# Product-key expert layer: own rooms for stored results, an earlier gate load, later index casts and one later exponential

## The chip, the cores and the metric

The kernel runs on one core of a Trainium2 chip. The metric is the device time of one execution in microseconds (us); the kernel before takes 2628.84 us, the median of 3 runs (2627.95 to 2629.35).

## The reference

The program is two transformer blocks on 512 tokens of width 1024. The change lies in the second half of the first block, the product-key layer (`peer_ffn`), which picks 16 of 16384 single-neuron experts per head and token:

```python
q = (xt @ w_query).reshape(T, H, 2, PEER_HALF)
s = jnp.einsum('thpd,hpkd->thpk', q, sub_keys).astype(f32)
top_s, top_i = lax.top_k(s, K)
cand_s = (top_s[:, :, 0, :, None] + top_s[:, :, 1, None, :]).reshape(T, H, K * K)
...
best_s, best_pos = lax.top_k(cand_s, K)
expert_idx = jnp.take_along_axis(cand_i, best_pos, axis=-1)
gate = jax.nn.softmax(best_s, axis=-1)
...
act = jnp.einsum('td,ted->te', x_blk, u[i_blk]).astype(f32)
hid = jax.nn.gelu(act, approximate=False) * g_blk
return jnp.einsum('te,ted->td', hid.astype(v.dtype), v[i_blk])
```

There are 8 heads, 128 keys for each half of a key, K = 16, and 16384 rows of 1024 in `u` and in `v`.

## The kernel before

The kernel is written in the order in which each engine executes (its schedule is manual): every engine takes its instructions strictly in program order, and waits where an operand or a room (a buffer of a pool) is not free yet. A DMA is issued from the queue of the engine that names it: `nc.sync` is SP, `nc.scalar` is ACT, `nc.gpsimd` is POOL.

**Weights.** Large matmuls are made of three: each operand is split into a high part and a rest, and `mm3` (L226 to L228) computes hi*hi, lo*hi and hi*lo. The class `Ring` brings the weights: `load` (L47, SP) fills one of 3 rooms `w_raw`, `split` copies the high part on ACT (L59, `w_hi`) and subtracts for the rest (L69, `w_lo`) on DVE, or on POOL where `pool=True`. A room of `w_raw` is free for the next load when `w_lo` has been computed. With `later=True` the subtraction is kept back until the next call of `next` or `split`.

**Tokens 128 to 511** (three tiles of 128) go the dense way: for each of the 128 blocks of 128 experts, a *u block* of 24 matmuls 128x384 gives the activations of all experts of the block (`act_steps`, 4 steps of 6 matmuls), ACT takes their gelu out of PSUM (L863), and later the expert loop multiplies by a dense gate and by the rows of `v`. Tokens 0 to 127 gather their experts' rows instead.

**`routes`** has three parts. (1) The query projection: 16 blocks on PE, each followed by `rank(b)`: 4 small matmuls of queries and keys into a PSUM tile `sm` of which there are two (L921), then DVE finds the 16 best with their indices (L924 to L932), and POOL casts the indices `ti` to `tib` (L933). (2) `choose(t, h0, h1)`: DVE works out the 16 best pairs of a head (21 pieces for 4 heads), with an exponential on ACT (L979) and, at the end, the indices `ik` (L1034). (3) `dispatch(t)` for t = 1, 2, 3: PE transposes `ik` and the gates (L1043 to L1045), and 32 rounds of one-hots and 8 matmuls each (L1081) build the dense gates, which ACT copies out of PSUM (L1082) and writes to DRAM in 24 writes `gd<-h` (L1088). `choose` of the next tile is woven between the rounds.

To keep PE busy, u blocks are fed in between: `steps(n)` adds n to an account and runs that many steps of u blocks. There are 4 steps between the last two ranks, 1.2 per piece of `choose(1, 4, 8)`, 2 + 32 x 1.2 in each `dispatch`. What is left of the 43 fed blocks is run at the end of `routes` (`drain(u_x)`), then two more. The results of the first 8 blocks go to `rows`, of the next 26 to `ge`, and of the last 11 to a tile `ga` of 2 rooms in `routes`' own pool `r_wk`, from which POOL writes them to DRAM (`away<-ga`, L866).

**`experts`** starts with a new pool `e_wk` in the space that `routes` gave back: POOL clears `acc` (L1143) and issues the load of the first gate tile, 1536 KB (`gate_tile(0)`, `gg<-gd`, L1147). `hidden(b)` multiplies gelu and gate on DVE (`hg`, L1187), splits the product into `hh` on ACT (L1188) and `hl` on DVE (L1189), and block b's 18 matmuls `o` read them.

Of the kernel before, what the change touches and what calls it, by code (L numbers as in the profile page):

```python
# [11 lines left out]
F32 = mybir.dt.float32  # L12
# [3 lines left out]
U32 = mybir.dt.uint32  # L16
# [6 lines left out]
NT = 4  # L23
# [5 lines left out]
class Ring:  # L29
# [49 lines left out]
    def next(self, ahead=2, pool=False, later=False):  # L79
        i = self.pos  # L80
        self.flush()
        self.load(i + self.depth)
        self.split(i + 1 + ahead, pool, later)
        self.pos += 1
        return self.hl.pop(i)
# [138 lines left out]
def mm3(nc, out, a, b, start, stop):  # L224

    nc.tensor.matmul(out, a[0], b[0], start=start, stop=False)  # L226
    nc.tensor.matmul(out, a[0], b[1], start=False, stop=False)  # L227
    nc.tensor.matmul(out, a[1], b[0], start=False, stop=stop)  # L228
# [12 lines left out]
def proj_fm(k, ps, nblk, xT, evac, pool=False, cuts=1):  # L241

    nc = k.nc
    for b in range(nblk):
        hi, lo = (w.rearrange("p (c f) -> p c f", c=KD) for w in k.ring.next(pool=pool, later=cuts > 1))
        p = ps.tile([128, T], F32, name="mm")
        for c in range(KD):
            mm3(nc, p, (hi[:, c], lo[:, c]), xT(c), c == 0, c == KD - 1)
            if c < KD - 1 and (c + 1) % (KD // cuts) == 0:
                yield  # L250
                if c + 1 == 2 * (KD // cuts):
                    k.ring.flush()
        evac(b, p)
        yield
# [19 lines left out]
def by_row(xT):  # L274

    return lambda c: tuple(x[:, c, :] for x in xT)
# [19 lines left out]
def drain(*gens):  # L296
    for g in gens:
        for _ in g:
            pass
# [482 lines left out]
LAG = 27 + LEAD  # L782

AWAY = 10
N = 384
# [30 lines left out]
def peer(k, h, xT, pools, parts, first):  # L816


    nc, tc, A = k.nc, k.tc, k.A
    with ExitStack() as ctx:  # L820
        ep = lambda name, bufs, **kw: ctx.enter_context(tc.tile_pool(name=name, bufs=bufs, **kw))
        s = Peer()
        s.one = one = ep("p2_one", 1)
        s.gep = ep("p2_ge", LAG - LEAD + 1)
        s.gat = k.rows
        s.pa = pools[0]
        s.gd = ep("p2_dram", 1, space=DRAM).tile([16, 128, NCH, 8 * CH], F32, name="gd")
        s.hd = ep("p2_hd", 1, space=DRAM).tile([128, NT, D], F32, name="hd")
        away = [ep(f"p2_away{i}", 1, space=DRAM).tile([128, N], F32, name="away") for i in range(AWAY + 1)]
        s.xT = xT  # L830
        s.n0 = one.tile([128, D], F32, name="n0")
        s.idx = one.tile([128, 128], I32, name="idx")
        s.g0 = one.tile([128, 128], F32, name="g0")
        s.act0 = one.tile([128, 128], F32, name="act0")
        s.ge, s.nact = {}, 0

        def act_steps(later=False):

            n = s.nact
            if n == 128:  # L840
                return
            if n >= LAG - 1 and n - LAG + 1 in s.away:
                ge = s.gep.tile([128, N], F32, name="ge")
                nc.sync.dma_start(out=ge, in_=s.away.pop(n - LAG + 1))
                s.ge[n] = ge
                s.nact += 1
                return
            uh, ul = (x.rearrange("p (c i) -> p c i", c=KD) for x in k.ring.next(later=later))
            p = s.pa.tile([128, 512], F32, name="mm")
            for c in range(KD):  # L850
                mm3(nc, p[:, 0:N], (uh[:, c], ul[:, c]), (s.xT[0][:, c, 128:512], s.xT[1][:, c, 128:512]), c == 0, c == KD - 1)
                if c % 2 and c < KD - 1:
                    yield
            if s.nact < LEAD:

                if s.nact % 2 == 0:
                    s.two = s.gat.tile([128, D], F32, name="rows")
                ge = s.two[:, s.nact % 2 * N:s.nact % 2 * N + N]
            elif s.wk is not None and n >= LAG - 1:
                ge = s.wk.tile([128, N], F32, name="ga")  # L860
            else:
                ge = s.gep.tile([128, N], F32, name="ge")
            nc.scalar.activation(ge, p[:, 0:N], AF.Gelu)  # L863
            if s.wk is not None and n >= LAG - 1:
                s.away[n - LAG + 1] = away[n - LAG + 1]
                nc.gpsimd.dma_start(out=away[n - LAG + 1], in_=ge)  # L866
            else:
                s.ge[n] = ge
            s.nact += 1
        s.act_steps = act_steps  # L870
        s.act = lambda later=False: drain(act_steps(later))
        s.away, s.wk = {}, None
        with ExitStack() as c2:
            routes(k, h, c2, s, pools[1], first)
        s.wk, s.nact = None, LAG - 1
        parts[1].close()
        return experts(k, s)


def routes(k, h, c2, s, ps, first):  # L880
    nc, tc, A = k.nc, k.tc, k.A
    ep = lambda name, bufs, **kw: c2.enter_context(tc.tile_pool(name=name, bufs=bufs, **kw))
    r1 = ep("r_one", 1)
    s.wk = wk = ep("r_wk", 2)
    s1 = ep("r_sm", 2, space=PSUM)
    s2 = ep("r_g", 2, space=PSUM)
    xT = s.xT
# [9 lines left out]
    for b in range(0, 16, 3):  # L897
        kt = s.gep.tile([128, 3, 128], F32, name="ge")
        n = min(3, 16 - b)
# [9 lines left out]
    tib = r1.tile([128, NT, 16, 16], BF, name="tib")  # L909
# [3 lines left out]
    def ev(b, p):  # L913
        qs[b] = wk.tile([128, T], F32, name="oa", bufs=4)
        nc.scalar.activation(qs[b], p, AF.Copy)

    def rank(b):
        q = qs.pop(b)
        sc = s1.tile([128, NT, 128], F32, name="sm")
        for t in range(NT):  # L920
            nc.tensor.matmul(sc[:, t, :], q[:, t * 128:(t + 1) * 128], keys[b], start=True, stop=True)  # L921
        rep = wk.tile([128, NT, 128], F32, name="ob", bufs=3)
        for t in range(NT):
            nc.vector.max(tv[:, t, b, 0:8], sc[:, t, :])  # L924
        for t in range(NT):
            nc.vector.match_replace(out=rep[:, t, :], in_to_replace=tv[:, t, b, 0:8], in_values=sc[:, t, :], imm_value=-3e38)
        for t in range(NT):
            nc.vector.max(tv[:, t, b, 8:16], rep[:, t, :])
        ti = wk.tile([128, NT, 16], U32, name="ti")
        for t in range(NT):  # L930
            nc.vector.max_index(ti[:, t, 0:8], tv[:, t, b, 0:8], sc[:, t, :])
            nc.vector.max_index(ti[:, t, 8:16], tv[:, t, b, 8:16], rep[:, t, :])  # L932
        nc.gpsimd.tensor_copy(tib[:, :, b, :], ti)  # L933
    gates, picks = {}, {}

    def choose(t, h0=0, h1=8, calm=None):
# [154 lines left out]
    def feed():  # L1091

        while s.nact < LAG + AWAY - 2:
            for i, _ in enumerate(s.act_steps()):
                if i == 1:
                    k.ring.split(k.ring.pos + 3, later=True)
                yield
            yield
    u_x, due = feed(), [0]

    def steps(n):
        due[0] += n
        while due[0] >= 1:
            due[0] -= 1
            next(u_x, None)


    for b in range(2):
        p, w = first[b]
        half_block(k, p, w, xT, 1)  # L1110
        ev(b, p)
        if b:
            rank(0)
    side = choose(1, 0, 4)
    for b, _ in enumerate(proj_fm(k, ps, 14, by_row(xT), lambda b, p: ev(b + 2, p), pool=True)):
        rank(b + 1)
        for _ in range(4 if b > 6 else 0):
            next(side, None)
    k.ring.split(k.ring.pos + 3, pool=True)
    steps(4)  # L1120
    rank(15)
    drain(side)
    for i, _ in enumerate(choose(1, 4, 8)):
        steps(1.2)
    for t in range(1, NT):
        calm = []
        weave(dispatch(t, calm), choose((t + 1) % NT, calm=calm), 1)
    drain(u_x)
    while s.nact < LAG + AWAY:
        s.act()  # L1130


def experts(k, s):
    nc, tc, A = k.nc, k.tc, k.A
    with ExitStack() as ctx:
        ep = lambda name, bufs, **kw: ctx.enter_context(tc.tile_pool(name=name, bufs=bufs, **kw))
        AHEAD, LAST, ROWS = 8, 125, 100 + LEAD
        wk = ep("e_wk", 2)
# [44 lines left out]
        def hidden(b):  # L1183
            ge = s.ge.pop(b)
            hg = wk.tile([128, N], F32, name="hg")
            hi, lo = (wk.tile([128, N], FR, name=n) if b <= LAST else s.gep.tile([128, N], FR, name="ge") for n in ("hh", "hl"))
            nc.vector.tensor_mul(hg.rearrange("p (c t) -> p c t", c=NCH), ge.rearrange("p (c t) -> p c t", c=NCH), gg[b // 8][:, :, b % 8, :])  # L1187
            nc.scalar.activation(hi, hg, AF.Copy)  # L1188
            nc.vector.tensor_sub(lo, hg, hi)  # L1189
            hid[b] = (hi, lo)  # L1190
        hidden(0)
        s.act()
        for b in range(LAST):
            if b % 8 == 2 and b < 120:
# [32 lines left out]
        for b in range(LAST + 1, 128):  # L1227
            hidden(b)
# [1010 lines left out]
```

## Time and profile before

| | |
|---|---|
| median of 3 runs | 2628.84 us |
| the profiled execution | 2629.32 us |
| its span | 2627.5 us |
| PE busy | 2561.2 us, 97% of the span |
| DVE busy | 1668.3 us, 63% |
| ACT busy | 940.1 us, 36% |
| POOL busy | 579.7 us, 22% |

The profile is one execution. A row of the timeline shows when an instruction started, how long it took, and in brackets how long its engine had been idle and which instruction released it. A stretch of the windows view shows busy time of every engine and the clock that TensorE (PE) was granted, 1.00 being 2.4 GHz and 0.50 being 1.2 GHz. With PE busy for nearly the whole span, time is found in the few places where it is idle or at the lower clock.

### The profile page before, as it was taken

How to read it: one execution, taken by the hardware profiler on the slowest of the kernel's cores; microseconds unless marked ns; L12 is line 12 of the kernel's file. 1: busy time of each engine (PE TensorE's matmuls, PEld its weight loads, DVE VectorE, ACT ScalarE, POOL GpSimd, SP SyncE). 2: the span in 40 equal slices, each digit the busy share in tenths (PEclk: the TensorE clock that was granted, in tenths of full speed). 3: DMA queues.
4: the chain of work that ended last, by engine and by line, in shares of the span. 5: the costliest groups of instructions: out<-in, count | busy, mean ns of one | idle time of the engine just before them, and what ended most of it. 6: DMA issues, size and time to landing. Idle time of an engine off the chain costs nothing.

```text
span 2627.5 us, 35859 instructions
## 1 busy us (share of the span) xinstructions
PE 2561.2 (97%) x13350; PEld 2037.8 (78%) x13350; DVE 1668.3 (63%) x3269; ACT 940.1 (36%) x1662; POOL 579.7 (22%) x485
## 2 busy tenths in 40 slices
PE   9999989997999999999999999999999999998997
PEld 7778889997789999999998778788888864453543
DVE  6446899993688887888888663555565552332223
ACT  5324237773333333333333443555422321110112
POOL 3200322222145555444443030111000110000000
PEclk9999999999999999999999999999999999999999
DMA  4223235666799999899898532222232579999996
GB/s 134 65 94 103 92 105 169 187 198 213 256 332 333 331 332 332 323 332 331 332 335 317 201 117 93 73 74 72 98 119 88 200 294 398 409 409 409 409 409 256
DMA packets 207952, 615.96 MB, mean 234 GB/s; under 512 B 18151, under 2 KB 69528, under 8 KB 205216
## 3 DMA queue, kind: packets, MB, share of 16 engines
q1 hardware_dynamic: 117808, 437.37, 44.8%
q0 software_dynamic: 38848, 142.71, 15.2%
q10 hardware_dynamic: 51120, 33.56, 4.4%
q8 instruction: 106, 1.74, 0.3%
q14 instruction: 70, 0.57, 0.1%
HBM read 579.95 MB, written 33.62 MB: 234 GB/s over the span
## 4 chain that ended last, share of the span: by engine, by line
PE 69%; DVE 4%; ACT 1%; DMA 1%; issue 1%; DVEq 0%; ACTq 0%; POOLq 0%; POOL 0%
PE mm L226 8%; PE mm L228 8%; PE mm L227 8%; PE o L226 6%; PE o L228 6%; PE o L227 6%; PE y L2035 4%; PE up L2014 4%; PE gate L2014 4%; PE pc L2046 2%; PE sc L226 1%; PE sc L227 1%; PE sc L228 1%; PE gate L1853 1%; PE up L1853 1%; PE po L1516 1%
## 5 line engine op out<-in xcount | busy, mean ns | idle before, releaser
L226 PE MATMUL mm<-nT_hi,w_hi 128*128 128x384 f32 (+1 forms) x1624 | 594.0, 366 | 2.4 <-ACT rows L863 2.3
L228 PE MATMUL mm<-nT_hi,w_lo 128*128 128x384 f32 (+1 forms) x1624 | 579.8, 357 | 2.7 <-POOL w_lo L69 2.7
L227 PE MATMUL mm<-nT_lo,w_hi 128*128 128x384 f32 (+1 forms) x1624 | 578.1, 356 | 0.0
L69 DVE TENSOR_TENSOR w_lo<-w_raw,w_hi 128x1024 fp32r<-128x1024 f32 x366 | 453.5, 1241 | 143.6 <-ACT w_hi L59 143.1
L59 ACT ACTIVATE w_hi<-w_raw 128x1024 fp32r<-128x1024 f32 x392 | 403.7, 1050 | 85.6 <-DMA w_raw<-in_peer_uT_dram 26.1
L226 PEld LDWEIGHTS mm<-nT_hi,w_hi 128*128 128x128 f32 x1624 | 306.4, 189 | 31.3 <-issue 3.6
L228 PEld LDWEIGHTS mm<-nT_hi,w_lo 128*128 128x128 f32 x1624 | 305.7, 188 | 28.0 <-POOL w_lo L69 3.7
L227 PEld LDWEIGHTS mm<-nT_lo,w_hi 128*128 128x128 f32 x1624 | 306.6, 189 | 24.8
L226 PE MATMUL o<-w_hi,hh 128*128 128x512 f32 x756 | 296.1, 392 | 17.9 <-ACT hh L1188 17.9
L228 PE MATMUL o<-w_hi,hl 128*128 128x512 f32 x756 | 297.6, 394 | 0.0
L227 PE MATMUL o<-w_lo,hh 128*128 128x512 f32 x756 | 296.7, 392 | 0.0
L863 ACT ACTIVATE ge<-mm 128x384 f32<-128x384 f32 x109 | 53.3, 489 | 429.3 <-PE mm L228 429.3
L226 PEld LDWEIGHTS o<-w_hi,hh 128*128 128x128 f32 x756 | 142.6, 189 | 48.3 <-ACT hh L1188 20.9
L228 PEld LDWEIGHTS o<-w_hi,hl 128*128 128x128 f32 x756 | 142.4, 188 | 31.9 <-DVE hl L1189 2.1
L227 PEld LDWEIGHTS o<-w_lo,hh 128*128 128x128 f32 x756 | 142.4, 188 | 28.0
L1189 DVE TENSOR_TENSOR hl<-hg,hh 128x384 fp32r<-128x384 f32 x126 | 70.7, 561 | 128.4 <-ACT hh L1188 128.4
L2021 DVE SCALAR_TENSOR_TENSOR ncT<-up,tw,ncT 128x512 f32<-128x512 f32 x16 | 12.0, 751 | 175.0 <-PE up L2014 175.0
L1153 POOL DMA_INDIRECT rows<-in_peer_u_dram,idx x64 | 91.6, 1431 | 121.6 <-DVE rows L1160 81.2
L2041 DVE SCALAR_TENSOR_TENSOR yl<-y,tw,yh 128x512 fp32r<-128x512 f32 x32 | 24.0, 751 | 144.9 <-ACT yh L2038 144.1
L1153 POOL DMA_INDIRECT h<-in_peer_u_dram,idx x64 | 90.9, 1420 | 105.9 <-DVE h L1160 95.2
L1188 ACT ACTIVATE hh<-hg 128x384 fp32r<-128x384 f32 x126 | 65.5, 519 | 134.3 <-DVE hg L1187 95.5
L1153 POOL DMA_INDIRECT h<-in_peer_v_dram,idx x64 | 82.6, 1291 | 106.2 <-DVE acc L1165 88.5
(732 smaller groups left out, 4680.4 us busy)
## 6 DMA issues: line engine op xcount, KB each, us to landing
w_raw<-in_peer_uT_dram SPq DMA_DIRECT2D x128, 512.0 KB
w_raw<-in_peer_v_dram SPq DMA_DIRECT2D x128, 512.0 KB
gd<-h ACTq DMA_DIRECT2D x24, 1024.0 KB
gg<-gd SPq DMA_DIRECT2D x15, 1536.0 KB
qk<-in_w_gate_dram SPq DMA_DIRECT2D x30, 512.0 KB
qk<-in_w_down_dram SPq DMA_DIRECT2D x28, 512.0 KB
qk<-in_w_up_dram SPq DMA_DIRECT2D x26, 512.0 KB
w_raw<-in_w_conv_dram SPq DMA_DIRECT2D x24, 512.0 KB
```

What stands on the lines that cost most here:

```text
L59: nc.scalar.activation(hi, w, AF.Copy)
L69: e.tensor_sub(lo, w, hi)
L226: nc.tensor.matmul(out, a[0], b[0], start=start, stop=False)
L227: nc.tensor.matmul(out, a[0], b[1], start=False, stop=False)
L228: nc.tensor.matmul(out, a[1], b[0], start=False, stop=stop)
L863: nc.scalar.activation(ge, p[:, 0:N], AF.Gelu)
L1153: nc.gpsimd.indirect_dma_start(out=r, out_offset=None, in_=A["peer_u"] if i < 128 else A["peer_v"], in_offset=bass.IndirectOffsetOnAxis(ap ...
L1188: nc.scalar.activation(hi, hg, AF.Copy)
L1189: nc.vector.tensor_sub(lo, hg, hi)
L1853: nc.tensor.matmul(p[:, i, 0:n], a[:, t, f], P[:, t, 0:n], start=i + t + j == 0, stop=t == NT - 1 and j == 1, skip_group_check=True)
L2014: nc.tensor.matmul(po[nm][r * 64:r * 64 + 64, :], xT[:, q * 2 + c, r * 64:r * 64 + 64], w[r][:, c * 512:c * 512 + 512], start=q == 0 and c ...
L2035: nc.tensor.matmul(py[i][r * 64:r * 64 + 64, :], aT[:, q, r * 64:r * 64 + 64], w[:, c * 512:c * 512 + 512], start=q == 0, stop=q == 3, ski ...
```

## The change

It has five parts.

- `ga` gets a pool of its own, `p2_ga`, with 2 rooms, that stays when `routes` ends. The flag `s.early` takes the place of the test on `s.wk`.
- The rest of the fed u blocks no longer runs at the end of `routes` but in `experts`, behind `gate_tile(0)`; `hidden(0)` stands ahead of the last u block.
- One u block more is fed among the ranks: 4 steps stand ahead of each of the ranks 14 and 15, where there were 4 steps between them only. For the two subtractions of weights in these steps `pool=s.slow` names POOL.
- The cast of rank b's indices is issued when rank b + 3 reaches its own (`turned(2)`), and the last three behind rank 15 (`turned()`); `ti` has 4 rooms.
- The exponential of `choose(1, 4, 8)` is kept back and issued two pieces later.

```diff
--- before.py
+++ after.py
@@ -823,6 +823,7 @@
         s.one = one = ep("p2_one", 1)
         s.gep = ep("p2_ge", LAG - LEAD + 1)
         s.gat = k.rows
+        ga = ep("p2_ga", 2)
         s.pa = pools[0]
         s.gd = ep("p2_dram", 1, space=DRAM).tile([16, 128, NCH, 8 * CH], F32, name="gd")
         s.hd = ep("p2_hd", 1, space=DRAM).tile([128, NT, D], F32, name="hd")
@@ -856,12 +857,12 @@
                 if s.nact % 2 == 0:
                     s.two = s.gat.tile([128, D], F32, name="rows")
                 ge = s.two[:, s.nact % 2 * N:s.nact % 2 * N + N]
-            elif s.wk is not None and n >= LAG - 1:
-                ge = s.wk.tile([128, N], F32, name="ga")
+            elif s.early and n >= LAG - 1:
+                ge = ga.tile([128, N], F32, name="ga")
             else:
                 ge = s.gep.tile([128, N], F32, name="ge")
             nc.scalar.activation(ge, p[:, 0:N], AF.Gelu)
-            if s.wk is not None and n >= LAG - 1:
+            if s.early and n >= LAG - 1:
                 s.away[n - LAG + 1] = away[n - LAG + 1]
                 nc.gpsimd.dma_start(out=away[n - LAG + 1], in_=ge)
             else:
@@ -869,10 +870,9 @@
             s.nact += 1
         s.act_steps = act_steps
         s.act = lambda later=False: drain(act_steps(later))
-        s.away, s.wk = {}, None
+        s.away, s.early = {}, True
         with ExitStack() as c2:
             routes(k, h, c2, s, pools[1], first)
-        s.wk, s.nact = None, LAG - 1
         parts[1].close()
         return experts(k, s)
 
@@ -881,7 +881,7 @@
     nc, tc, A = k.nc, k.tc, k.A
     ep = lambda name, bufs, **kw: c2.enter_context(tc.tile_pool(name=name, bufs=bufs, **kw))
     r1 = ep("r_one", 1)
-    s.wk = wk = ep("r_wk", 2)
+    wk = ep("r_wk", 2)
     s1 = ep("r_sm", 2, space=PSUM)
     s2 = ep("r_g", 2, space=PSUM)
     xT = s.xT
@@ -926,11 +926,18 @@
             nc.vector.match_replace(out=rep[:, t, :], in_to_replace=tv[:, t, b, 0:8], in_values=sc[:, t, :], imm_value=-3e38)
         for t in range(NT):
             nc.vector.max(tv[:, t, b, 8:16], rep[:, t, :])
-        ti = wk.tile([128, NT, 16], U32, name="ti")
+        ti = wk.tile([128, NT, 16], U32, name="ti", bufs=4)
+
+        turned(2)
         for t in range(NT):
             nc.vector.max_index(ti[:, t, 0:8], tv[:, t, b, 0:8], sc[:, t, :])
             nc.vector.max_index(ti[:, t, 8:16], tv[:, t, b, 8:16], rep[:, t, :])
-        nc.gpsimd.tensor_copy(tib[:, :, b, :], ti)
+        last.append((tib[:, :, b, :], ti))
+    last = []
+
+    def turned(but=0):
+        while len(last) > but:
+            nc.gpsimd.tensor_copy(*last.pop(0))
     gates, picks = {}, {}
 
     def choose(t, h0=0, h1=8, calm=None):
@@ -1093,7 +1100,7 @@
         while s.nact < LAG + AWAY - 2:
             for i, _ in enumerate(s.act_steps()):
                 if i == 1:
-                    k.ring.split(k.ring.pos + 3, later=True)
+                    k.ring.split(k.ring.pos + 3, pool=s.slow, later=True)
                 yield
             yield
     u_x, due = feed(), [0]
@@ -1113,21 +1120,28 @@
             rank(0)
     side = choose(1, 0, 4)
     for b, _ in enumerate(proj_fm(k, ps, 14, by_row(xT), lambda b, p: ev(b + 2, p), pool=True)):
-        rank(b + 1)
+        if b < 13:
+            rank(b + 1)
         for _ in range(4 if b > 6 else 0):
             next(side, None)
     k.ring.split(k.ring.pos + 3, pool=True)
-    steps(4)
-    rank(15)
+    s.slow = True
+    for b in (14, 15):
+        steps(4)
+        rank(b)
+    s.slow = False
+    turned()
     drain(side)
-    for i, _ in enumerate(choose(1, 4, 8)):
+    exps, n = [], 0
+    for _ in choose(1, 4, 8, exps):
+        n += len(exps)
+        if exps and n == 3:
+            exps.pop()()
         steps(1.2)
     for t in range(1, NT):
         calm = []
         weave(dispatch(t, calm), choose((t + 1) % NT, calm=calm), 1)
-    drain(u_x)
-    while s.nact < LAG + AWAY:
-        s.act()
+    s.u_x = u_x
 
 
 def experts(k, s):
@@ -1188,7 +1202,13 @@
             nc.scalar.activation(hi, hg, AF.Copy)
             nc.vector.tensor_sub(lo, hg, hi)
             hid[b] = (hi, lo)
+
+        drain(s.u_x)
+        while s.nact < LAG + AWAY - 1:
+            s.act()
         hidden(0)
+        s.act()
+        s.early, s.nact = False, LAG - 1
         s.act()
         for b in range(LAST):
             if b % 8 == 2 and b < 120:
```

The diff shows the code; the order of the instructions on POOL moves in two places. On **POOL at the last ranks** (the projection's end, up to the first one-hot of `dispatch(1)`; L933 is the cast of rank indices) before:

```order
L69 TENSOR_TENSOR w_lo<-w_raw,w_hi 128x1024
L933 CAST tib<-ti 128x4x16
L69 TENSOR_TENSOR w_lo<-w_raw,w_hi 128x1024
L933 CAST tib<-ti 128x4x16
L69 TENSOR_TENSOR w_lo<-w_raw,w_hi 128x1024
L933 CAST tib<-ti 128x4x16
L1064 TENSOR_TENSOR oa<-eq,pT 128x512 x46
```

and with the change (the cast is L940, the one-hot L1071):

```order
L69 TENSOR_TENSOR w_lo<-w_raw,w_hi 128x1024 x2
L940 CAST tib<-ti 128x4x16
L69 TENSOR_TENSOR w_lo<-w_raw,w_hi 128x1024
L940 CAST tib<-ti 128x4x16 x4
L69 TENSOR_TENSOR w_lo<-w_raw,w_hi 128x1024
L1071 TENSOR_TENSOR oa<-eq,pT 128x512 x44
```

Before, each subtraction stands behind the cast of the rank just issued, and the last one here belongs to u block 2; now the subtractions of u blocks 3 and 4 are POOL's too, and the last stands behind the casts of the ranks 12 to 15.

On **POOL at the end of `routes`** (L866 writes stored u results away, L1147 loads the first gate tile) before:

```order
L866 DMA away<-ga 128x384
L1064 TENSOR_TENSOR oa<-eq,pT 128x512
L866 DMA away<-ga 128x384 x9
L1143 MEMSET acc 128x1024
L1147 DMA gg<-gd 128x3072
L1153 DMA h<-in_peer_u_dram,idx 128x1024 x4
```

and with the change:

```order
L1071 TENSOR_TENSOR oa<-eq,pT 128x512
L867 DMA away<-ga 128x384
L1157 MEMSET acc 128x1024
L1161 DMA gg<-gd 128x3072
L867 DMA away<-ga 128x384 x7
L1167 DMA h<-in_peer_u_dram,idx 128x1024 x4
```

The clearing of `acc` and the gate load have moved ahead of seven of the eleven writes; the gathers of expert rows stay behind the last of them.

## Rows read from the trace of the kernel before

**Rows 1.** PE timeline: start us, duration us, engine, line, operation, [idle before <-releaser]

```profile
348.29 0.39 PE L228 MATMUL mm<-nT_hi,w_lo 128*128 128x512 f32 x1
...
350.23 1.13 PE L921 MATMUL sm<-ge,oa 128*128 128x128 f32 x8 [1.56 <-DVE ti L931]
...
351.12 0.42 PE L226 MATMUL mm<-nT_hi,w_hi 128*128 128x384 f32 x1
...
383.01 0.33 PE L226 MATMUL mm<-nT_hi,w_hi 128*128 128x384 f32 x1
...
387.17 0.33 PE L226 MATMUL mm<-nT_hi,w_hi 128*128 128x384 f32 x1
...
392.36 0.27 PE L1043 MATMUL mm<-ident,ik 128*128 128x128 f32 x1
```

**Rows 2.** Windows: stretch, its us, busy per engine, granted PE clock, DMA share, GB/s

```profile
348.50:392.50 44.00, 36.33 (x193) 34.91 (x193) 40.05 (x187) 15.95 (x20) 9.62 (x7) 0.92 0.37 119
392.50:610.50 218.00, 214.85 (x1499) 211.58 (x1498) 208.44 (x526) 161.69 (x356) 52.58 (x51) 1.00 0.63 184
659.10:664.40 5.30, 5.29 (x13) 4.13 (x14) 3.27 (x5) 1.47 (x2) 0.94 (x1) 0.50 0.90 315
```

**Rows 3.** Waits of PE over the span: us in total, times, longest us

```profile
PE mm L228 <- POOL w_lo L69: 2.7, 2, 1.4
PE mm L226 <- ACT rows L863: 2.3, 1, 2.3
```

**Rows 4.** Timeline of ACT, then of POOL, then of ACT, 326 to 376 us

```profile
336.39 1.05 ACT L59 ACTIVATE w_hi<-w_raw 128x1024 fp32r<-128x1024 f32 x1
...
326.81 2.41 POOL L69 TENSOR_TENSOR w_lo<-w_raw,w_hi 128x1024 fp32r<-128x1024 f32 x1 [2.56 <-ACT w_hi L59]
...
340.95 2.37 POOL L69 TENSOR_TENSOR w_lo<-w_raw,w_hi 128x1024 fp32r<-128x1024 f32 x1
...
350.41 0.24 POOL L933 CAST tib<-ti 128x64 bf16<-128x64 uint32 x1 [7.08 <-DVE ti L932]
...
350.60 2.40 POOL L69 TENSOR_TENSOR w_lo<-w_raw,w_hi 128x1024 fp32r<-128x1024 f32 x1
...
375.06 0.26 ACT L979 ACTIVATE gt<-gt 128x64 f32<-128x64 f32 x1 [3.02 <-DVE gt L977]
```

**Rows 5.** DVE timeline, 328 to 390 us

```profile
328.93 0.28 DVE L932 FIND_INDEX8 ti<-tv,ob 128x8 uint32<-128x128 f32 x1
...
341.06 2.34 DVE L1020 TENSOR_TENSOR gt<-gt,gs 128x64 f32<-128x64 f32 x1
...
350.27 3.35 DVE L1012 TENSOR_TENSOR oh<-oh 128x256 bf16<-128x256 bf16 x4
...
368.19 0.75 DVE L955 TENSOR_TENSOR cand<-tv 128x64 f32<-128x64 f32 x5
...
381.56 0.23 DVE L1020 TENSOR_TENSOR gt<-gt,gs 128x64 f32<-128x64 f32 x1
...
388.84 1.23 DVE L69 TENSOR_TENSOR w_lo<-w_raw,w_hi 128x1024 fp32r<-128x1024 f32 x1 [1.02 <-ACT w_hi L59]
...
389.98 0.35 DVE L1034 TENSOR_TENSOR ik<-oh 128x64 f32<-128x64 bf16 x2
```

**Rows 6.** PE timeline at the start of the expert loop

```profile
642.40 0.34 PE L228 MATMUL mm<-nT_hi,w_lo 128*128 128x384 f32 x1
659.11 0.79 PE L226 MATMUL o<-w_hi,hh 128*128 128x512 f32 x1 [16.38 <-ACT hh L1188]
```

**Rows 7.** Timeline of ACT, POOL and DVE, 611 to 658 us, one or two rows each

```profile
611.15 0.37 ACTq L1088 DMA_DIRECT2D gd<-h  x1
...
643.61 0.54 POOL L866 DMA_DIRECT2D away<-ga  x1 [3.62 <-ACT ga L863]
...
647.09 0.54 POOL L1147 DMA_DIRECT2D gg<-gd  x1
...
657.94 0.56 DVE L1187 TENSOR_TENSOR hg<-rows,gg 128x384 f32<-128x384 f32 x1 [16.59 <-DMA gg<-gd]
```

## The prediction

> **What bounds the kernel now.** I first read the busy times of the engines: PE works nearly all the time, so only stretches in which it stands still, or runs at the lower clock, can give time back. PE's list of waits and the windows then show two such stretches in the code of this change.
>
> *The first* lies between the end of the query projection and the first transposes of `dispatch(1)`. PE starts the last projection matmul at 348.29 and the transposes at 392.36 [rows 1], about 43.8 us after the former's end. What it does there has a price in the same view: a u block takes 4.16 us (383.01 to 387.17, 24 matmuls), the group of matmuls of a rank 0.89 us (350.23 to 351.12). In between stand two ranks and 29 steps, 4 by `steps(4)` and 25 by 1.2 a piece, a step being a quarter of a block: 29 x 1.04 + 2 x 0.89 = 32.0 us. So **11.8 us** are lost. The window agrees: PE is busy 36.33 of 44.00 us, thus idle for 7.7, and its granted clock of 0.92 accounts for most of the rest [rows 2]. PE waits here for subtractions `w_lo` on POOL (2.7 us in two waits), for PSUM behind a gelu (2.3 us) [rows 3], and for DVE before rank 14 (1.56 us) [rows 1].
>
> Why POOL is late stands in the fourth group. The high part of u block 0 was made at 336.39 to 337.44 on ACT, yet POOL subtracts only at 350.60, since a cast stands ahead of it that had to wait for DVE's indices until 350.41 [rows 4]. Why ACT is late: the exponential waited 3.02 us for DVE and started at 375.06 [rows 4], and the gelu that PE needs stands behind it.
>
> *The second* is the start of the expert loop. The last u matmul starts at 642.40, the first `o` matmul at 659.11 [rows 6]: with a spacing of 0.17 us (4.16/24), 16.5 us of standing still. After it PE runs for 5.30 us at clock 0.50 [rows 2], which costs half of that, 2.65. Together **19.2 us**. The cause is an order: the gate load is issued at 647.09, behind the last write `away` at 643.61, and DVE gets to `hg` at 657.94, released by that load [rows 7].
>
> **The change part by part.** PE's matmuls are the same in number and size; they are only moved. What can change is waits.
>
> *Gate load first, own rooms.* The load now stands ahead of the last u blocks. Of its 172 fed steps the routes code consumes 33 + 3 x 40.4 = 154; so 18 steps or 4.4 blocks are left at its end, and with blocks 43 and 44 that is 6.4 blocks or 27 us of PE work. `acc` and the gate tile no longer lie where `ga` lay, so they wait for no write of `ga`, only for the end of `routes`. When does the load land? It must wait for the last write `gd<-h`, issued at 611.15 [rows 7]; by the first stretch that is about 6 us earlier, 605. How long that write takes to land no row shows: from 0 to, at most, what the gate load itself took in its crowded queue, 657.94 - 647.09 = 10.9 us [rows 7]. Add 1 us to clear `acc` and 10.9 for the load: 617 to 628, and 1.2 us for `hg` and `hh` (657.94 to 659.11 [rows 6, 7]). PE will need `hh` at 642.6 less the gain of the first stretch, about 632. Margin 3 to 14 us, so all 19.2 us go. What is queued behind the moved work: on POOL seven writes `away` stand behind the gate load; while it waits, two rooms of `ga` and two PSUM tiles take up four blocks, 16.6 us of PE time, more than the 12 us by which it can be late. On DVE and ACT `hidden(0)` now stands ahead of the gelu of block 44; with the load long landed it costs them about a microsecond beside PE's work. SP has the same order; its load of the second gate tile loses its wait for `ga`, and nothing is added.
>
> *One u block more among the ranks; casts later.* PE's demand for rank 14 comes one block, 4.16 us, later, which covers the 1.56. POOL's subtractions for blocks 0 to 3 wait for no fresh cast: the casts ahead of them are three ranks old. So the 2.7 us go, and with them loads that were held back because `w_raw` was not free. POOL's new order has one weak place: the subtraction for block 4 stands behind the casts of the ranks 12 to 15. DVE ends rank 15 at 368.19 now (its next instruction [rows 5]), with the change at about 364.0 (below); cast 0.24 and subtraction 2.4 [rows 4] make 366.7. PE arrives at block 4's first use of it at 348.6 + 2 x (4.16 + 0.89) + 2 x 4.16 + 0.35 = 367.4. Just in time.
>
> *DVE.* The transposes need `ik`, ready at 390.33 [rows 5]. Twice in the ranks DVE stands still beside a subtraction of POOL that began just before: at 341.06 an operation takes 2.34 us that takes 0.23 at 381.56, and at 350.27 four others take 3.35 [rows 5], beside POOL's 340.95 and 350.60 [rows 4]. Rank operations don't suffer: 0.28 us at 328.93 [rows 5] beside POOL's 326.81 to 329.22 [rows 4]. With the casts out of the way these subtractions start when ACT has the high part, which falls among rank operations: 2 x 2.1 = 4.2 us less. Between rank 15 and `ik` DVE has six subtractions of weights where it had seven: 1.2 us less; an idle time of 1.02 behind a late `w_hi` [rows 5] goes too. Against it stands block 4's subtraction on POOL, which begins just when DVE starts `choose` with sums of two tiles: up to 2.4 us more, or nothing; I take 2.4, since the rows at 341 and 350 are the nearest. The Trainium skill (SBUF — State Buffer, section Who interferes with whom) has this as a rule: a VectorE instruction with two SBUF inputs and a GpSimd instruction that reads SBUF exclude each other for a whole instruction. It speaks against moving subtractions to POOL; by it the sum below is 29.4, without it 31.0, and rows 5 agree with it at both places.
>
> So `ik` is ready at 390.33 - 4.2 - 1.2 - 1.0 + 2.4 = 386.3. PE reaches the transposes, without waits, at 392.36 - 11.8 + 4.16 = 384.7, and waits 1.6. The first stretch gives 11.8 - 1.6 = **10.2 us**. Bounds: 11.8, if DVE is ahead, and 6.0, if DVE gains nothing (390.5).
>
> *Exponential two pieces later.* Two pieces are 2.4 steps or 2.5 us of PE's time, and DVE's input comes earlier by about 3; the 3.02 us wait on ACT goes, and with it PE's 2.3, counted in the 11.8. Its two table loads remain, once each.
>
> *`dispatch`* keeps its order, and u blocks keep their place in it, since exactly one whole block moved. POOL gets one write more there and two one-hots' places shift: nothing. PE is idle for 3.15 of 218.00 us [rows 2]; at best these go too.
>
> **Sum:** 19.2 + 10.2 = 29.4. The profiled execution took 2629.3 us, 0.5 above the median of 2628.84; 2629.3 - 29.4 = 2599.9, and set against the median **2599.4**. The span would be 2598.1.
>
> **Rivals.**
> - *DVE stays the bound of the first stretch.* If the subtractions of POOL meet other operations of DVE and nothing is won there, `ik` comes at 390.5, PE waits 5.8 in place of 1.6, and block 4's subtraction is 3 us late within that. The gain is 6.0, or about 3 with another half-clock stretch as after the second gap (2.65): 2603.6 to 2606.3. For it: DVE is busy 40.05 of 44.00 us [rows 2]. Against it: both stalls have POOL's late subtraction beside them. Chance 0.17.
> - *The gate load still ends late.* If the last `gd` write or shared rooms hold it, part of the 19.2 stays, at most all: 2606 to 2618.6. For it: 1536 KB took 10.9 us. Against it: that was beside gathers, which still come behind the last write. Chance 0.07.
> - *Nothing moves:* another wait stands behind each one removed, within 5.3 us of now. PE has slack in neither stretch, so both would have to fail: 0.05.
> - *Slower.* `hidden(0)` stands in DVE's and ACT's queue ahead of the subtractions and gelus of the last blocks. If the gate tile landed late enough, these would stand behind it, loads would stop for want of `w_raw` rooms, and PE would begin `o` at landing + 1.2 and run dry after two blocks. It is slower from a landing at about 658 on, and by more than 5.3 from 663; at 668, 2639. The load would need some 50 us against 10.9. Chance 0.04.
>
> **How the numbers follow.** The forecast has 0.67, with a range of its own from 2594.5 (all of 19.2 + 11.8 and the 3.15 idle in `dispatch`) to 2603. About 0.2% or 5.3 us is what a measurement of this kernel can tell from no change. Faster: 0.67 + 0.17 + 0.07 = 0.91; same 0.05; slower 0.04. The range from 2594.5 to 2609 takes in the first rival and a part of the second, and leaves out less than 2 in 10.
>
> **What would show it.** Right: the first `o` matmul follows the last u matmul with no wait for `hh`, and the granted clock there is 1.00; the gate load is issued some 20 us before the last u matmul; the two waits for POOL's `w_lo` and the one for the gelu are gone; from the last projection matmul to the transposes about 38 us pass, with one u block more inside. DVE's operations of 2.34 us at `choose(1, 0, 4)` are short. Wrong: a wait of PE's transposes of several us for `ik`, a new wait for `w_lo` in block 4, DVE idle at `hg` while subtractions stand behind it, or a wait of gelu for a room of `ga`.

## The result and the profile after

| | before | after |
|---|---|---|
| median of 4 runs each | 2628.64 us | 2610.32 us |
| lowest to highest | 2627.95 to 2629.35 | 2610.04 to 2611.55 |
| span of the profiled execution | 2627.5 | 2608.3 |
| last projection matmul to the transposes of `ik` | 44.07 | 43.02, with a u block of 4.16 more in it |
| transposes to the last `pg` group (`dispatch`) | 217.07 | 217.16 |
| last `pg` group to the first `o` matmul | 49.68 | 35.99, with that block less |
| first `o` matmul to the end | 1968.4 | 1963.7 |

The ratio is 0.9931, with a 95% interval from 0.9919 to 0.9943: faster, by 18.3 us, where 29.4 were forecast and the range ended at 2609. In equal work, and in this pair of executions, the first stretch gave 44.07 - 43.02 + 4.16 = 5.2 us and the second 49.68 - 35.99 - 4.16 = 9.5; behind the first `o` came 4.7.

PE's timeline of the kernel after, the counterpart of [rows 1, 6]:

```profile
348.41 0.39 PE L228 MATMUL mm<-nT_hi,w_lo 128*128 128x512 f32 x1
...
360.76 1.13 PE L921 MATMUL sm<-ge,oa 128*128 128x128 f32 x8 [2.71 <-issue]
...
373.96 0.44 PE L228 MATMUL mm<-nT_hi,w_lo 128*128 128x384 f32 x1 [1.80 <-POOL w_lo L69]
...
391.43 0.27 PE L1050 MATMUL mm<-ident,ik 128*128 128x128 f32 x1
...
608.59 1.05 PE L1088 MATMUL pg<-ob,oa 128*128 128x128 f32 x8
...
629.28 0.69 PE L226 MATMUL mm<-nT_hi,w_hi 128*128 128x384 f32 x1 [4.03 <-ACT ga L864]
...
644.40 0.33 PE L228 MATMUL mm<-nT_hi,w_lo 128*128 128x384 f32 x1
644.58 0.39 PE L226 MATMUL o<-w_hi,hh 128*128 128x512 f32 x1
```

The first `o` matmul now follows the last u matmul without a wait; the 16.38 us of [rows 6] are gone. But a wait of 4.03 us has come among the last u blocks, at 629.28, for a gelu. In the first stretch two waits have taken the place of those in [rows 1, 3]: 2.71 us before rank 15 and 1.80 for a `w_lo` of POOL. The windows of the same kernel (stretch, its us, busy per engine, granted PE clock, DMA share, GB/s), as in [rows 2]:

```profile
348.50:391.50 43.00, 38.48 (x217) 37.80 (x216) 41.39 (x195) 17.42 (x22) 8.99 (x8) 0.96 0.33 108
391.50:608.50 217.00, 213.83 (x1490) 210.51 (x1489) 208.59 (x526) 161.60 (x356) 52.59 (x51) 1.00 0.63 186
629.30:635.20 5.90, 5.90 (x19) 5.90 (x20) 2.92 (x3) 2.20 (x3) 1.08 (x2) 0.50 0.60 194
644.50:649.80 5.30, 5.30 (x25) 4.40 (x24) 2.77 (x4) 2.93 (x5) 3.28 (x4) 1.00 0.68 209
```

The half clock has moved too: the expert loop begins at 1.00 (last row, before 0.50), and the 5.90 us behind the new wait run at 0.50, which costs 2.95. The new wait with its clock is thus worth 4.03 + 2.95 = 7.0 us. In the first stretch 43.00 - 38.48 = 4.52 us are idle, which are the two waits, and DVE is busy for 41.39 of 43.00. Behind the wait of 2.71 the clock is 0.67 over 5.24 us (360.76 to 366.00), which costs another 1.7; so this stretch loses 6.2 us.

Where the new wait comes from stands in POOL's timeline of the kernel after (L1157 clears `acc`, L1161 loads the first gate tile, L867 writes a stored u result away):

```profile
609.76 0.95 POOL L1157 MEMSET acc<- 128x1024 f32 x1 [0.64 <-DMA w_raw<-in_peer_uT_dram]
620.08 0.54 POOL L1161 DMA_DIRECT2D gg<-gd  x1 [9.37 <-DMA w_raw<-in_peer_v_dram]
620.61 1.10 POOL L867 DMA_DIRECT2D away<-ga  x2
```

and in ACT's (L864 is the gelu, L1095 the write `gd<-h`):

```profile
610.31 0.37 ACTq L1095 DMA_DIRECT2D gd<-h  x1
612.80 0.49 ACT L864 ACTIVATE ga<-mm 128x384 f32<-128x384 f32 x1 [1.58 <-PE mm L228]
...
616.96 0.49 ACT L864 ACTIVATE ga<-mm 128x384 f32<-128x384 f32 x1 [2.72 <-PE mm L228]
...
628.73 0.49 ACT L864 ACTIVATE ga<-mm 128x384 f32<-128x384 f32 x1 [10.33 <-DMA away<-ga]
```

The load is issued at 620.08, 9.8 us after the last `gd` write that it reads behind (the row names a weight load as the releaser; releasers are inferred). In the first experiment below, whose profile has the landings, that write is issued at 610.63 and lands 8.4 us later, and the load is issued 0.5 us after that. Two gelus fill the two rooms of `ga`; the third has to wait until a write `away`, issued at 620.61 behind the load, has landed at 628.73. Until then PE fills two PSUM tiles and stops.

The first stretch is read on DVE and POOL, as in [rows 4, 5]. DVE's timeline of the kernel after:

```profile
331.01 1.11 DVE L999 TENSOR_TENSOR cand<-one,cand 128x64 uint32<-128x64 uint32 x1
...
332.22 2.39 DVE L1002 TENSOR_SCALAR cand<-cand 128x64 uint32<-128x64 uint32 x1
...
344.37 2.62 DVE L1019 TENSOR_TENSOR oh<-oh 128x512 bf16<-128x512 bf16 x1
...
351.66 4.51 DVE L1019 TENSOR_TENSOR oh<-oh 128x256 bf16<-128x256 bf16 x4
...
360.37 0.29 DVE L933 FIND_INDEX8 ti<-tv,sm 128x8 uint32<-128x128 f32 x1
...
370.75 0.74 DVE L962 TENSOR_TENSOR cand<-tv 128x64 f32<-128x64 f32 x5
...
390.19 0.35 DVE L1041 TENSOR_TENSOR ik<-oh 128x64 f32<-128x64 bf16 x2
```

and POOL's:

```profile
329.63 2.40 POOL L69 TENSOR_TENSOR w_lo<-w_raw,w_hi 128x1024 fp32r<-128x1024 f32 x1
...
332.17 2.39 POOL L69 TENSOR_TENSOR w_lo<-w_raw,w_hi 128x1024 fp32r<-128x1024 f32 x1
...
344.17 2.54 POOL L69 TENSOR_TENSOR w_lo<-w_raw,w_hi 128x1024 fp32r<-128x1024 f32 x1 [3.77 <-ACT w_hi L59]
350.51 2.39 POOL L69 TENSOR_TENSOR w_lo<-w_raw,w_hi 128x1024 fp32r<-128x1024 f32 x1 [3.81 <-ACT w_hi L59]
...
353.11 2.46 POOL L69 TENSOR_TENSOR w_lo<-w_raw,w_hi 128x1024 fp32r<-128x1024 f32 x1
...
370.89 0.70 POOL L940 CAST tib<-ti 128x64 bf16<-128x64 uint32 x1 [4.49 <-DVE ti L934]
371.55 2.35 POOL L69 TENSOR_TENSOR w_lo<-w_raw,w_hi 128x1024 fp32r<-128x1024 f32 x1
```

DVE's stalls have not gone, they have moved to other instructions: each lies beside a subtraction of POOL that began before it (the last beside two). In the kernel before there were three as well, the two of [rows 5] and one ahead of them, again beside a subtraction (DVE's timeline, then POOL's):

```profile
331.23 2.35 DVE L997 TENSOR_TENSOR abf<-cand 128x64 bf16<-128x64 uint32 x1
...
331.10 2.39 POOL L69 TENSOR_TENSOR w_lo<-w_raw,w_hi 128x1024 fp32r<-128x1024 f32 x1
```

Set against the same operations undisturbed (0.23, 0.23 and 1.19 us; after 0.22, 0.19, 0.42 and 1.19), the stalls cost 6.4 us before and 8.6 after. So DVE ends rank 15 at 370.75 (next instruction; 368.19 in [rows 5]), and `ik` starts at 390.19 where it started at 389.98. PE doesn't wait for `ik`: it is ready at 390.54, and PE comes to the transposes without a wait at 391.43. What it waits for stands earlier. The matmuls of rank 15 at 360.76 follow DVE's last read of the `sm` of rank 13 (360.37 + 0.29), since there are two rooms of `sm`; and the `w_lo` of the 1.80 us is POOL's subtraction at 371.55, behind the cast that waited for DVE's rank 15.

### The profile page after: what moved, and what is told of

It reads as the page before. It is cut to its first block, busy times and chain, and to the rows that moved or that the text cites. A ratio compares the mean times of both kernels' runs of the same rounds, so it can differ in the third digit from the quotient of the medians.

```text
span 2608.3 us, 35852 instructions
## 1 busy us (share of the span) xinstructions
PE 2557.0 (98%) x13350; PEld 2037.6 (78%) x13350; DVE 1668.6 (64%) x3267; ACT 939.7 (36%) x1662; POOL 584.7 (22%) x487
## 5 line engine op out<-in xcount | busy, mean ns | idle before, releaser
L864 ACT ACTIVATE ge<-mm 128x384 f32<-128x384 f32 x109 | 53.2, 488 | 427.7 <-PE mm L228 427.6
L69 POOL TENSOR_TENSOR w_lo<-w_raw,w_hi 128x1024 fp32r<-128x1024 f32 x28 | 68.2, 2440 | 250.1 <-ACT w_hi L59 241.1
```

Source lines behind the costliest of these rows:

```text
L69: e.tensor_sub(lo, w, hi)
```

## The experiments

Two questions: what is the 4.03 us wait for, rooms or transfers (theories 1 and 2), and what holds the first stretch, the stalls of DVE beside POOL (called the lock) or DVE's own work (theories 3 and 4). Times are medians of four runs (ten for the fourth), each with its ratio to the kernel before on the same chip (medians 2628.21 to 2628.43).

**1. Four rooms of `ga` in place of two.**

```diff
-        ga = ep("p2_ga", 2)
+        ga = ep("p2_ga", 4)
```

> The changed kernel with 4 rooms of ga in place of 2, nothing else. Theory 1 (the rooms): in the changed kernel the gate load stands on POOL ahead of the writes of stored u results and waits 9.4 us for the last gd write; the two rooms of ga are full by then, the third gelu waits until the first write has landed (628.7), and PE waits 4.0 us and then runs 5.9 us at half clock, 7 us together. With 4 rooms that wait is gone: about 2603.3 us, PE's wait on ga 0. Theory 2 (the transfers): the gate load and the gate writes fill the DMA engines and whatever PE needs comes late; more rooms change nothing: 2610, a wait of about 4 us stays, on a gelu or on a weight load.

Measured: 2605.2 us, ratio 0.9915 [0.9898, 0.9932]. From the last `pg` group to the first `o` matmul 28.97 us pass, 7.02 fewer than after. The window of this kernel over the place of the wait shows PE busy throughout, at full clock:

```profile
608.00:638.00 30.00, 30.00 (x178) 30.00 (x177) 9.41 (x10) 10.22 (x16) 5.30 (x9) 1.00 0.92 318
```

although the gate load is as late as in the kernel after. POOL's timeline, then DVE's:

```profile
619.57 0.54 POOL L1161 DMA_DIRECT2D gg<-gd  x1 [8.54 <-DMA w_raw<-in_peer_v_dram]
...
628.61 0.56 DVE L1201 TENSOR_TENSOR hg<-rows,gg 128x384 f32<-128x384 f32 x1 [0.30 <-DMA gg<-gd]
```

So the wait was for rooms, and the load itself, landing at 628.6, is 9.3 us ahead of the first `o` at 637.88. The median fell by 5.1 us and not by 7. In this execution, the fastest of its four, the time fell by 6.7, although the first stretch took 44.6 us against 43.0 with the same code in it: its second wait (1.97 us) was followed by a clock of 0.50 over 3.19 us, where the clock behind the 1.80 us of the kernel after was 1.00. Such a difference between executions is as large as the 1.9 us that are missing; which of them explains the median isn't shown.

**2. The first gate load from SP in place of POOL.**

```diff
-            (nc.sync if g8 else nc.gpsimd).dma_start(...)
+            nc.sync.dma_start(...)
```

> The changed kernel with the first gate load issued from SP in place of POOL; 2 rooms of ga. Theory 1 (POOL's order): the writes no longer stand behind the gate load, rooms come free in time, the 4.0 us wait is gone: about 2603.5 us, as with 4 rooms, unless SP, which now waits for the last gd write itself, brings weights of v too late (slack about 20 us by the changed trace, so no). Theory 2 (the transfers): the same bytes at the same time, 2610, wait stays.

Measured: 2610.62 us, ratio 0.9938 [0.9921, 0.9954]: nothing gained. SP's timeline of this kernel shows why:

```profile
596.32 0.33 SPq L47 DMA_DIRECT2D w_raw<-in_peer_uT_dram  x1
614.70 0.33 SPq L1161 DMA_DIRECT2D gg<-gd  x1
615.09 1.91 SPq L47 DMA_DIRECT2D w_raw<-in_peer_uT_dram  x3
```

SP came to the load behind its weight load of 596.32 and could issue it only at 614.70, 5.7 us after the last `gd` write was issued (608.99; it landed after 5.6), and three weight loads stood behind it. ACT's next high part then waited (its timeline):

```profile
622.77 1.06 ACT L59 ACTIVATE w_hi<-w_raw 128x1024 fp32r<-128x1024 f32 x1 [10.79 <-DMA w_raw<-in_peer_uT_dram]
```

and the gelu behind it too, so PE stood still for 4.48 us up to 624.25. The writes were free (one issued at 612.27 landed after 2.7 us), the weights were late. A wait moved to another queue is a wait for what is queued there.

**3. The gate part alone, and 4. the rest alone** (a block more among the ranks, later casts, later exponential). Core of the two diffs against the kernel after:

```diff
-    s.slow = True
-    for b in (14, 15):
-        steps(4)
-        rank(b)
...
+    steps(4)
+    rank(15)
```

```diff
-        drain(s.u_x)
-        while s.nact < LAG + AWAY - 1:
-            s.act()
         hidden(0)
-        s.act()
```

> The change's gate part alone: own rooms for ga, gate load ahead of the last u blocks; the ranks, the casts and the exponential as before. By the two traces this part removes 19.2 us and adds about 7 (wait for ga and half clock): about 12 less than before, 2616.6 us, with the transposes of dispatch(1) at 392.4 as before. If the parts are not additive (the gate part profits from the earlier dispatch): 2618 or more.

> The other half alone: one u block more among the ranks with two subtractions on POOL, later casts, later exponential; gate load and ga as before. By the traces the loss of the first stretch falls from 11.8 to about 6.7: 5 less than before, 2623.6 us; the wait of the first o matmul for hh stays at 16 us. The forecast's own number for this half was 10.2: 2618.4.

Measured: the gate part 2614.17 us, ratio 0.9948 [0.9931, 0.9964]; the rest 2624.54 us, ratio 0.9984 [0.9974, 0.9994]. That is 14.0 us (2.4 more than expected) and 3.7, together 17.7 of the 18.3: within the intervals, of some 4 and 2.5 us, the parts add up. PE's waits in the fourth kernel keep the old wait for `hh`:

```profile
PE o L226 <- ACT hh L1204: 17.8, 3, 16.3
```

**5. POOL without subtractions** (the first kernel, in which ACT copies in POOL's place from the eighth projection block on).

```diff
-            e.tensor_sub(lo, w, hi)
+            if self.copy and e is self.k.nc.gpsimd:
+                self.k.nc.scalar.activation(lo, w, AF.Copy)
+            else:
+                e.tensor_sub(lo, w, hi)
```

> The changed kernel with 4 rooms of ga, and from the 8th of the 14 projection blocks on, up to u block 4, POOL subtracts no rests of weights: ACT copies the weight into w_lo in its place (the rest is left out, so the numbers are another product). Theory 3 (the lock): in the changed kernel DVE's sums beside POOL's subtractions still take 2.39, 2.62 and 4.51 us where 0.2, 0.4 and 1.0 are normal, about 8 us together, so DVE ends rank 15 at 370.8 and PE waits 2.7 for rank 15 and 1.8 for the rest of block 4. Without POOL's subtractions these DVE operations are short, rank 15 ends near 363, both waits go, the transposes come at about 386, and the time falls from 2605.2 to about 2599.5. Theory 4 (DVE's own work, not the lock, is the bound of this stretch): DVE's times stay, ranks end at 370, 2605.

Measured: 2591.58 us, ratio 0.9862 [0.9845, 0.9878]. The stretch takes 36.4 us against 44.6 in the first kernel. Its window shows PE without a gap and at full clock:

```profile
348.30:384.60 36.30, 36.30 (x216) 36.26 (x215) 33.05 (x163) 20.02 (x25) 1.23 (x3) 1.00 0.37 117
```

DVE has the same rank work, and no instruction of it from 328 to 368 us takes longer than 1.23 us. So DVE's own work does not bound the stretch; what POOL's subtractions add to it does. The total is 5.4 us below what these eight microseconds account for, since 5.9 us more are gained behind the first `o` (1957.9 us to the end against 1963.8). They belong to the edit: nothing resets its flag, so the three subtractions that POOL does at the end of the expert loop (1514.95 to 1528.4 in the first kernel) are copies on ACT as well. From the first `o` to the end of that place 904.6 us pass against 909.9 in the first kernel, which is 5.3 of the 5.9. So of this kernel only the first stretch counts here, not the total.

**6. The casts not delayed, and 7. the exponential not delayed** (each the first kernel with one part undone).

```diff
-        turned(2)
...
+        turned()
```

```diff
-    for _ in choose(1, 4, 8, exps):
+    for _ in choose(1, 4, 8):
```

> The changed kernel with 4 rooms of ga, but each cast of rank indices right behind its rank as before. If the later casts are what keeps the rests of u blocks 0 to 2 in time, PE waits for w_lo again (2.7 us and some half clock): 2608 to 2609. If they brought nothing, since POOL's subtractions only meet DVE at other places (theory 3), 2605 or a little less.

> The changed kernel with 4 rooms of ga, but the exponential of choose(1, 4, 8) where it stood before. By the forecast's reason the gelu of a u block stands behind the exponential again and PE waits 2 to 3 us: about 2608. By the changed trace the exponential still waits 2.96 us for DVE while PE does not wait for its gelu, so there is some slack: at the least 2605.

Measured: 2604.3 us, ratio 0.9908 [0.9892, 0.9925], and 2604.56 us, ratio 0.9909 [0.9892, 0.9925], against 2605.2 with all parts. Neither delay brings anything. Without the delayed casts PE has other waits (4.03 and 1.09 us for `w_lo`), and DVE has the stalls of the kernel before, as its timeline of the sixth kernel shows:

```profile
331.17 2.35 DVE L1004 TENSOR_TENSOR abf<-cand 128x64 bf16<-128x64 uint32 x1
...
341.01 2.35 DVE L1027 TENSOR_TENSOR gt<-gt,gs 128x64 f32<-128x64 f32 x1
...
350.21 3.34 DVE L1019 TENSOR_TENSOR oh<-oh 128x256 bf16<-128x256 bf16 x4
```

but the stretch takes 43.6 us, between the 43.0 and 44.6 of the delayed form: in both, PE waits for something that DVE is late with. Without the delayed exponential PE's waits are those of the kernel after, 2.71 and 1.80 us, and none for a gelu.

**8. A block more still ahead of rank 15** (on the first kernel).

```diff
+        if b == 15:
+            s.slow = False
+            steps(4)
```

> The changed kernel with 4 rooms of ga and 8 steps in place of 4 ahead of rank 15 (still two subtractions on POOL, the third on DVE). DVE starts rank 15 only at 366.0 and PE could give its matmuls up to then, so one more u block fills the wait of 2.7 us and what follows at half clock; the rest of block 4 no longer stands behind the last casts, so its wait of 1.8 goes too. About 4 less: 2601. Against it: the gate load has one u block less to hide behind; if it lands late, a wait for hh of up to 4 us takes the gain back: 2605.

Measured: 2601.8 us, ratio 0.99 [0.9883, 0.9916]. The wait before rank 15 falls to 0.62 us, and 2.12 for a subtraction on DVE remain, so 3.4 of the block's 4.16 us are won: a stretch that DVE bounds takes PE's work almost for nothing.

**9. The subtraction tied to the next rank.** A mark of one element per partition, written by DVE behind the four pieces of `choose(1, 0, 4)` that follow a rank and copied by POOL, lets POOL's subtraction begin only when DVE has the next rank's operations before it (on the first kernel).

```diff
+        if 6 < b < 13:
+            m = [wk.tile([128, 1], F32, name=n) for n in ("m1", "m2")]
+            nc.vector.memset(m[0], 0.0)
+            nc.gpsimd.tensor_copy(m[1], m[0])
```

> The changed kernel with 4 rooms of ga and a mark: behind the four pieces of choose(1, 0, 4) that follow a rank, DVE writes one number per partition, and POOL copies it ahead of its next subtraction of a rest. POOL then begins that subtraction when DVE turns to the next rank, whose operations the lock has not slowed in any trace. All arithmetic is as in the changed kernel. Theory 3 (the lock): DVE's 2.39, 2.62 and 4.51 us operations become short, the interval from the last projection matmul to the transposes falls from 44.6 to about 37 to 39 us, 2605.2 becomes about 2598 to 2600. Against it: POOL's subtractions come up to 8 us later, as DVE lags PE; if PE then waits for them, the interval stays at 42 to 44 and the time at 2603 to 2605. If the lock were not the cause (theory 4): 2605.

Measured: 2599.02 us (2598.05 to 2599.71), ratio 0.989 [0.9872, 0.9907]; all of its runs lie below all of the first kernel's (2603.63 to 2606.03). POOL's timeline of this kernel, one of six such pairs:

```profile
340.70 0.19 POOL L1130 COPY m<-m 128x1 f32<-128x1 f32 x1 [4.83 <-DVE m L1129]
340.84 2.37 POOL L69 TENSOR_TENSOR w_lo<-w_raw,w_hi 128x1024 fp32r<-128x1024 f32 x1
```

and DVE's:

```profile
345.24 1.19 DVE L1019 TENSOR_TENSOR oh<-oh 128x256 bf16<-128x256 bf16 x4
...
354.19 0.89 DVE L924 MAX8 tv<-sm 128x8 f32<-128x128 f32 x4 [2.61 <-PE sm L921]
...
364.09 0.75 DVE L962 TENSOR_TENSOR cand<-tv 128x64 f32<-128x64 f32 x5
...
383.52 0.35 DVE L1041 TENSOR_TENSOR ik<-oh 128x64 f32<-128x64 bf16 x2
```

The four operations that took 4.51 us take 1.19, rank 15 ends at 364.09, and the transposes come 36.98 us after the last projection matmul (348.16 to 385.14) with 36.2 us of work between them. DVE now waits for PE's scores (2.61 us ahead of rank 14, 0.31 ahead of rank 15) and no longer PE for DVE. PE's window:

```profile
348.50:385.10 36.60, 36.34 (x215) 35.92 (x214) 31.87 (x156) 17.52 (x22) 11.79 (x12) 1.00 0.46 145
```

**10. The mark and the block of the eighth kernel together** (the diffs of both).

> The same mark with 8 steps ahead of rank 15 (one more u block among the ranks). If the mark alone leaves no wait, this gives nothing, and the gate load has less to hide behind: 2598 to 2600, as with the mark alone. If a wait of PE for rank 15 or for a rest is left, it is filled: 2 us less than the mark alone, or against the run with 8 steps alone (2601.8) 3 us less.

Measured: 2598.6 us (2597.19 to 2600.09), ratio 0.9886 [0.9868, 0.9904], the same as with the mark alone. Once DVE no longer bounds the stretch, one more block in it buys nothing. Kernels 9 and 10 beat both the kernel before and the change.

## Why the prediction was right or wrong

**Right: the second stretch's old wait.** The wait for `hh` and the half clock behind it are gone. The load was issued 24 us before the last u matmul (620.08, 644.40), where some 20 were said, and landed at 628.6 in the first experiment, just behind the forecast's 617 to 628. With enough rooms, all that was forecast there came.

**Wrong: "two rooms of `ga` and two PSUM tiles take up four blocks, 16.6 us of PE time, more than the 12 us by which it can be late".** The 16.6 are right: PE ran dry at 629.28 - 4.03 = 625.25, 16.7 us after the last `pg` group at 608.59. The other side of the comparison is wrong. It ended where POOL *issues* the writes, but a room is free when its write has *landed*, and the write was in the queue behind 1536 KB: 628.73 - 620.61 = 8.1 us more. (In the first experiment the three writes ahead of the load land 2.3 to 6.0 us after their issue, the first behind it 9.3; in the second, where the load is not in that queue, all land after 2.2 to 7.6.) From 608.59 to the end of the gelu that got the room (628.73 + 0.49) are 20.6 us; less 16.7 that is the wait, 4.0. With the half clock 7.0 us, and experiment 1 gave back 7.02 in its trace.

**Wrong: "these subtractions start when ACT has the high part, which falls among rank operations: 2 x 2.1 = 4.2 us less".** The first half held: POOL's subtractions at 344.17 and 350.51 now wait for ACT's high part alone. The second did not: that moment fell on the sums and one-hots that stand between two ranks. The forecast had counted two stalls of before, 4.2 us, and taken both to go; it had overlooked the third, at 331.23. There were 6.4 us of stalls before and 8.6 after. So rank 15 ended at 370.75, 2.6 us later than before, where 364.0 was forecast, 4.2 earlier. The place where PE would pay was wrong too. The forecast had it wait 1.6 us for `ik` at the transposes. There it waited for nothing, but DVE's delay reached it earlier, 2.71 us before rank 15 and 1.80 at block 4, which had been called just in time; with the lower clock that is 6.2. What follows rank 15 came as worked out: from there to `ik` 19.44 us against 21.79 before, so 2.35 fewer, for which the six subtractions in place of seven and the idle time had been set at 2.2; the 2.4 set against them for block 4's subtraction on POOL were not charged, since it (371.55) fell beside MAX8 and FIND_INDEX8. With the stalls taken away by the mark, PE reached the transposes at 385.14, where 384.7 had been written for a PE that waits for nothing. That DVE then ended rank 15 at 364.09, and 364.0 had been forecast, is luck: the third stall was left out of the forecast, and so were DVE's waits for PE of 2.9 us, and the two nearly cancel. The step was a guess about the phase between two engines, and nothing in the rows of before fixed that phase.

The Trainium skill (SBUF — State Buffer, section Who interferes with whom) says that a DVE instruction with two SBUF inputs contends with a GpSimd instruction that reads SBUF, and that the order of issue decides who stands. The rows agree: 344.17 on POOL is ahead of 344.37 on DVE, and DVE ends at 346.99, just after POOL's 346.71. The prediction used the rule for the price of a stall; whether one would occur it settled by the guess.

**Casts and exponential.** The prediction had the 2.7 us of `w_lo` waits and the 2.3 behind the gelu vanish with these two edits. The waits did change, but experiments 6 and 7 price the edits at nothing, since PE pays for DVE's delay in either form, and the gelu's 2.3 us did not come back without the delay. The exponential itself still waits 2.96 us against 3.02 before; without its delay it waits 6.16 (experiment 7), so two pieces of delay were eaten by the later end of rank 15. The gain of the stretch came, it seems, with the block that was moved into it; experiment 8, where the next block brings 3.4, supports that, but that block was not undone by itself. The 5.2 us hold for one pair of executions, with clocks of 0.96 and 0.92 over the stretch. Against the 44.6 us of experiment 1, whose clock is 0.92 as before, it is 3.6, and experiment 4's medians give 3.7.

**The sum.** 29.4 less 7.0 for the rooms, less 5.0 (10.2 - 5.2) for the stalls, is 17.4. The profiled spans differ by 19.2. The 1.8 more lie behind the first `o`, where 4.7 us were gained and 2.65 foreseen (0.2 were lost ahead of it); that part of the program takes from 1963.7 to 1967.2 us in the kernels that do not wait for `hh` and compute the same numbers, so 1.8 is within what it varies by. The two mishaps had been thought of in part. "DVE stays the bound", with subtractions of POOL that meet other operations of DVE, is what came; it was priced at a gain of 6.0, or 3 with a half-clock stretch, though by a wait at the transposes. Its `ik` at 390.5 was met at 390.54 by luck: rank 15 was 2.6 us later than it had it, and what follows 2.35 shorter. A gelu's wait for a room of `ga` stood among the signs of being wrong, without a price. What was missing was both at once, 2599.4 + 5.0 + 7.0 = 2611.4, and so the range ended too early. Kernel 9, with both mishaps removed, took 2599.02 us.

## What to carry to other kernels

A buffer that is emptied by a DMA is free at the landing, so what covers a wait has to be counted to there, with everything that is ahead of the write in its queue. Where two engines stall each other, phase decides: what counts is which instruction of the one falls beside which of the other, and where that matters it can be set, here with a mark of one element that releases the subtraction when the other engine has harmless work. A stretch that one engine bounds takes other engines' work almost for nothing, but only until that engine is no longer the bound.

## What the runs showed of the hardware

- A TENSOR_SCALAR with one SBUF operand (128x64, uint32) stood for 2.39 us beside POOL's subtraction, against 0.19 us elsewhere. The prediction had looked only at instructions with two SBUF operands. The Trainium skill's section named above lists `tensor_scalar` among the operations that can take the shared ports; the row agrees. MAX8, FIND_INDEX8 and MATCH_REPLACE8 were not lengthened beside POOL's subtraction of 371.55 to 373.90 (0.68 us for four, 0.23 and 0.23 us each; in the kernel before 0.67, 0.24 and 0.23, with no subtraction on POOL).
- The last `gd` write of 1024 KB held the gate load for 9.8 us in the kernel after, and for 5.7 (608.99 to 614.70) in experiment 2, where SP issued no weight loads meanwhile; the DMA share over these stretches was 0.89 and 0.75.
- In the kernel after, a standstill of 2.71 us before rank 15 was followed by a granted clock of 0.67 over 5.24 us (1.00 until 362.0, 0.50 from 363.0 to 365.0), one of 4.03 by 0.50 over 5.90, one of 1.80 by 1.00 over 2.04. In experiment 1 the same code had its standstill of 1.97 us followed by 0.50 over 3.19.
